# Gate and up projection of an encoder block by Strassen's seven products instead of eight

## The chip, the cores and the metric

The kernel runs on one core of a Trainium2 chip. The metric is the device time of one execution in microseconds. A profile of one execution gives, for each engine, every instruction's start and length; TensorE (PE) multiplies, VectorE (DVE), ScalarE (ACT) and GpSimd (POOL) work element by element, SyncE (SP) issues the DMAs. PEld are PE's weight loads, which overlap its products.

## The reference

One layer of a hybrid encoder block, 512 tokens of width 1024, in float32. The part that changes is its last third:

```python
mixed = (g_attn * attn_out + g_ssd * ssd_out) @ w_out[i]
x = x + rms_norm(mixed, norm1_post[i])
h2 = rms_norm(x, norm2_pre[i])
gate, up = jnp.split(h2 @ w_gate_up[i], 2, axis=-1)      # 1024 -> 2 x 2816
ffn = (jax.nn.silu(gate) * up) @ w_down[i]               # 2816 -> 1024
x = x + rms_norm(ffn, norm2_post[i])
```

Ahead of it stand the input projection, attention and a state-space branch, whose code the change leaves as it is.

## The kernel before

Every matrix product is made of float32r products in three passes: each operand is split into a high part (a cast on ACT, line 150 for weights, 187 for activations) and a low part (the difference, line 152 on DVE or POOL, 188 on DVE), and low x high, high x low and high x high are added in PSUM (`mm3`, lines 182 to 184).

Weights come in chunks of 128 x 1024 through a ring of three buffers `raw`, and their parts lie in rings `whi` and `wlo` of four buffers each. `wnext` hands out chunks in the order of use and splits AHEAD = 2 of them early. Activations lie in rings of 2 KB slots (`SLOTS`: x, z, q, t). PSUM has eight banks, in four rings of two (sa, sb, mm, sc). A planner with a cost model sets the order of each engine's instructions from the order of the trace in which the program lists them and from their dependencies; within `manual_schedule` the named engines keep the listed order. Once set, an engine's order is fixed.

`out_proj` computes the output projection token tile by token tile (four tiles of 128) into all eight banks (`token_major8`); the last four of the eight k-tiles are done one token tile after the other, so each tile's epilogue (two squares on ACT, rstd, residual sum, gain) runs beside the next tile's products. The epilogue ends with `transpose_tile`, eight PE transposes whose results are split into h2T. The row factor rstd is left out of h2T and multiplied in later, as a row `rb` that PE spreads over the partitions.

`ffn` goes through 22 blocks of 128 features. A block has a gate chunk and an up chunk of weights; each is multiplied with h2T of all 512 tokens (`chan_major`, 8 k-tiles x 3 passes = 24 products of 512 columns). The first two blocks are done in halves of 256 tokens, so that they can begin while token tiles 2 and 3 are still in their epilogue; their first three weight chunks are held in ring q (NQW). `post` multiplies both results with rb, applies SiLU, multiplies, and splits the result for the next product. `down` is the last projection, again by `token_major8`, with 22 k-tiles.

Of the kernel before, what the change touches and what calls it, by code (L numbers as in the profile page):

```python
# [38 lines left out]
NQW = 3  # chunks of w_gu held in ring q  # L39
# [7 lines left out]

class Halves:
    """[P, 1024] held as two [P, 512] tiles; a slice of columns lies in one of them"""
# [10 lines left out]
class Block:  # L60
    def __init__(self, ctx, tc, a, out):
# [3 lines left out]
        self.cp = pool("cp", 1)  # L65
        self.wp = pool("wp", 3)
        self.bp = pool("bp", 4)
        self.sp = pool("sp", 1)
        self.tp = pool("tp", 6)
# [9 lines left out]
    SLOTS = {"x": 14, "z": 8, "q": 15, "t": 17}  # L79

    def slot(self, tag, shape, dt=F32, name="s"):
        """a tile of up to 2 KB per partition from one of the rings"""
        return self.sp.tile([P] + list(shape), dt, tag=tag, name=self.nm(name), bufs=self.SLOTS[tag])

# [13 lines left out]
    def weights(self):  # L98
        """every weight chunk in the order of use: (source, columns, engine of the low parts)"""
# [16 lines left out]
        for j in range(NF):  # L116
            for u in range(2):
                yield a["w_gu"][j + u * NF], 1024, "g" if j < 3 and j > 0 else "v", 2 * j + u < NQW
        for j in range(NF):
            yield a["w_dn"][j], 1024, "v"  # L120

    def wload(self):
        c = next(self.wseq, None)
        if c is not None:
            src, n, lo, *q = c
# [10 lines left out]
    def presplit(self):  # L136
# [12 lines left out]
        for c in cs:  # L149
            self.A.copy(h[:, c], raw[:, c])  # L150
# [692 lines left out]
    def token_major8(self, nk, ntail, lhs, epilogue):  # L843
# [230 lines left out]
```

## Time and profile before

| | us |
|---|---|
| median of 3 runs (lowest to highest) | 870.79 (867.84 to 872.43) |
| span of the profiled execution, first to last instruction | 862.0 |
| from the span to the lowest, median, highest run | 5.8, 8.8, 10.4 |

The profile is of one execution, of which the span is known; the runs' times contain what lies around the span as well. A term worked out from the profile changes the span, and the 8.8 us are taken over to the median.

### The profile page before, as it was taken

To read this page: it belongs to the slowest core of one execution; us is meant where nothing else is said; L and a number is where in the kernel's file an instruction comes from. 1 tells how busy PE (TensorE), PEld (TensorE's weight loads), DVE (VectorE), ACT (ScalarE), POOL (GpSimd) and SP (SyncE) were. 2 spreads that over 40 slices of the span, in tenths; PEclk is the share of its full clock that TensorE was granted. 3 is DMA by queue.
4 is the path that set the end of the run, shared out by engine and by line. 5 is a ranking of instruction groups with operands and counts; after the bars stand their busy time and mean duration, and the time that the engine had idled before them with its cause. 6 is when DMAs were issued, how large, how long until landed. Compare 5 with 4: busy or idle time off the path is not lost.

```text
span 862.0 us, 10158 instructions
## 1 busy us (share of the span) xinstructions
PE 833.0 (97%) x3886; PEld 666.3 (77%) x3886; DVE 489.9 (57%) x730; ACT 337.1 (39%) x571; POOL 210.9 (24%) x124
## 2 busy tenths in 40 slices
PE   9898998799999999999999999999999999999996
PEld 7786886566666777677888798888888888888885
DVE  3976489876436667687863845444444444322225
ACT  7554445655723332276234624333333333211122
POOL 3454451400444465459451200000000000000000
PEclk9999999999999999999999999999999999999999
DMA  9422220200322221157225522222222222422214
GB/s 314 159 102 98 74 83 17 98 0 1 111 98 87 97 98 62 49 188 264 98 98 160 187 94 95 91 91 97 95 96 96 98 99 97 147 98 98 98 49 146
DMA packets 33312, 91.12 MB, mean 106 GB/s; under 512 B 4208, under 2 KB 4592, under 8 KB 33264
## 3 DMA queue, kind: packets, MB, share of 16 engines
q1 hardware_dynamic: 33264, 90.48, 30.5%
q8 instruction: 30, 0.49, 0.2%
q14 instruction: 18, 0.15, 0.1%
HBM read 82.08 MB, written 8.39 MB: 105 GB/s over the span
## 4 chain that ended last, share of the span: by engine, by line
PE 77%; DVE 12%; ACT 4%; issue 3%; DMA 2%; POOL 1%; SPq 0%; DVEq 0%; ACTq 0%; POOLq 0%
PE mm L182 12%; PE mm L184 12%; PE mm L183 12%; PE sc L183 7%; PE sc L184 7%; PE sc L182 7%; DVE u L552 3%; PE sc L652 2%; PE sb L182 2%; PE sb L183 2%; PE sb L184 2%; PE sa L183 2%; PE sa L182 2%; PE sa L184 2%; PE sb L631 1%
## 5 line engine op out<-in xcount | busy, mean ns | idle before, releaser
L150 ACT CAST whi<-raw 128x1024 fp32r<-128x1024 f32 (+3 forms) x126 | 128.2, 1019 | 253.7 <-PE sc L184 122.8
L152 POOL TENSOR_TENSOR wlo<-raw,whi 128x1024 fp32r<-128x1024 f32 (+3 forms) x62 | 141.6, 2289 | 230.8 <-ACT whi L150 228.9
L152 DVE TENSOR_TENSOR wlo<-raw,whi 128x1024 fp32r<-128x1024 f32 (+1 forms) x64 | 78.1, 1220 | 110.9 <-ACT whi L150 110.9
L182 PE MATMUL mm<-hT,wlo 128*128 128x512 f32 x176 | 73.4, 417 | 0.0
L183 PE MATMUL mm<-hT,whi 128*128 128x512 f32 x176 | 69.5, 395 | 0.0
L184 PE MATMUL mm<-hT,whi 128*128 128x512 f32 x176 | 69.3, 394 | 0.0
L182 PE MATMUL mm<-h2T,wlo 128*128 128x512 f32 (+1 forms) x176 | 66.8, 379 | 0.0
L183 PE MATMUL mm<-h2T,whi 128*128 128x512 f32 (+1 forms) x176 | 66.8, 379 | 0.0
L184 PE MATMUL mm<-h2T,whi 128*128 128x512 f32 (+1 forms) x176 | 66.8, 379 | 0.0
L182 PE MATMUL sc<-h2T,wlo 128*128 128x512 f32 x160 | 62.7, 392 | 0.0
L184 PE MATMUL sc<-h2T,whi 128*128 128x512 f32 x160 | 62.3, 389 | 0.0
L183 PE MATMUL sc<-h2T,whi 128*128 128x512 f32 x160 | 62.2, 389 | 0.0
L182 PEld LDWEIGHTS mm<-hT,wlo 128*128 128x128 f32 x176 | 33.4, 190 | 9.1 <-issue 2.5
L183 PEld LDWEIGHTS mm<-hT,whi 128*128 128x128 f32 x176 | 33.2, 189 | 8.6 <-issue 2.4
L184 PEld LDWEIGHTS mm<-hT,whi 128*128 128x128 f32 x176 | 33.2, 189 | 7.4 <-issue 0.5
L182 PEld LDWEIGHTS mm<-h2T,wlo 128*128 128x128 f32 x176 | 33.1, 188 | 6.3
L183 PEld LDWEIGHTS mm<-h2T,whi 128*128 128x128 f32 x176 | 33.1, 188 | 6.3
L184 PEld LDWEIGHTS mm<-h2T,whi 128*128 128x128 f32 x176 | 33.1, 188 | 6.1
L743 DVE TENSOR_TENSOR E<-E,cb 128x512 f32<-128x512 f32 x16 | 28.6, 1788 | 11.4 <-ACT E L742 11.4
L183 PEld LDWEIGHTS sc<-h2T,whi 128*128 128x128 f32 x160 | 30.0, 188 | 6.5 <-issue 0.2
L182 PEld LDWEIGHTS sc<-h2T,wlo 128*128 128x128 f32 x160 | 30.0, 188 | 6.5 <-issue 0.2
L184 PEld LDWEIGHTS sc<-h2T,whi 128*128 128x128 f32 x160 | 30.0, 188 | 6.2
(374 smaller groups left out, 1912.8 us busy)
## 6 DMA issues: line engine op xcount, KB each, us to landing
raw<-in_w_gu SPq DMA_DIRECT2D x44, 512.0 KB, 3.2
raw<-in_w_dn SPq DMA_DIRECT2D x22, 512.0 KB, 3.3
raw<-in_w_g SPq DMA_DIRECT2D x16, 512.0 KB, 3.3
raw<-in_w_xbc SPq DMA_DIRECT2D x12, 512.0 KB, 3.4
raw<-in_w_z SPq DMA_DIRECT2D x8, 512.0 KB, 3.2
spd<-spill SPq DMA_DIRECT2D x16, 256.0 KB, 2.0
raw<-in_w_sp SPq DMA_DIRECT2D x8, 512.0 KB, 4.0
raw<-in_w_o SPq DMA_DIRECT2D x8, 512.0 KB, 3.2
```

What stands on the lines that cost most here:

```text
L150: self.A.copy(h[:, c], raw[:, c])
L152: e.tensor_tensor(l[:, c], raw[:, c], h[:, c].bitcast(F32), ALU.subtract)
L182: self.T.matmul(o, ll, rh, start=first, stop=False)
L183: self.T.matmul(o, lh, rl, start=False, stop=False)
L184: self.T.matmul(o, lh, rh, start=False, stop=last)
L552: self.tap[j] = V.scalar_tensor_tensor(u[:, lo_o : lo_o + n], p[:, lo_i : lo_i + n], self.cw[:, j, k : k + 1], u[:, lo_o : lo_o + n], ALU. ...
L631: self.T.transpose(pp[:, t * P : t * P + P], prs[t][:, k * P : k * P + P], self.ident)
L652: self.T.matmul(po[i * HD : i * HD + HD, :], self.vt[:, k, g * HD : g * HD + HD], pts[h - 1 + i][k], start=k == 0, stop=k == NT - 1)
L743: V.tensor_tensor(E, E, cb[:, 0].unsqueeze(1).to_broadcast([P, 4, P]), ALU.mult)
```

## The change

Write h2 (without its row factor) as A with blocks A11, A12 (tokens 0 to 255; k 0 to 511 and 512 to 1023), A21, A22 (tokens 256 to 511), and a block's weights as B11, B21 (gate, the two halves of k) and B12, B22 (up). The eight block products of AB become seven (Winograd's form of Strassen's algorithm):

- sums of weights per feature block: P1 = B11 + B12, P2 = P1 + B22, P3 = B12 + B22, P4 = P2 + B21 (P1, P3 on POOL, P2, P4 on DVE), each split into high and low parts afterwards
- sums of activations, once: R1 to R4 from A11, A12 and the transposes of tiles 2 and 3 (`blocks`), each split; low parts of R3, R2 and R1 on POOL
- products, each of 4 k-tiles x 3 passes with 256 columns (`product`): v = B21 A12, u = B11 A11, then u continued by P2 R2 and later by P1 R1, px = P3 R3 continued by P4 A22, pw = B22 R4. Between the continuations DVE and ACT read the partial sums.

PE's order is written out by hand for output projection and gate/up projection: a block's order is B21, B11, P1 of the block before, P3, B22, P2, P4. The first two products of blocks 0 and 1, which need tiles 0 and 1 alone, come before tile 3's transposes, and tile 2's lie among them. Further: tile t's transposes follow the next tile's products (`rest`); weights of gate/up are no longer split ahead through `wnext` and ring q; the products of SiLU and up are kept unsplit and split in `down`; up is not multiplied by rb, which is made good in the last epilogue by the factor r2; the rings x, z, q and the transposed activations end with the mixing, and rings e (25 slots) and A (14 of 4 KB) take their place.

```diff
+        self.mp = pool("mp", 1)
+        self.early = ExitStack()
+        self.bp = self.early.enter_context(tc.tile_pool(name="bp", bufs=4))
+        self.sp = self.early.enter_context(tc.tile_pool(name="sp", bufs=1))
...
-    SLOTS = {"x": 14, "z": 8, "q": 15, "t": 17}
+    SLOTS = {"x": 14, "z": 8, "q": 15, "t": 17, "e": 25}
...
-        for j in range(NF):
-            for u in range(2):
-                yield a["w_gu"][j + u * NF], 1024, "g" if j < 3 and j > 0 else "v", 2 * j + u < NQW
-        for j in range(NF):
-            yield a["w_dn"][j], 1024, "v"
...
+        rest = None
         for t in range(NT):
             for n in range(2):
                 for k in range(nk - ntail, nk):
                     one(k, t, n)
-            epilogue(t, po[t])
+            if rest:
+                rest()
+            rest = epilogue(t, po[t])
+        return rest
...
+        self.blk = {n: [self.sp.tile([P, 4, 256], F32R, tag="A", name=self.nm(n), bufs=14) for _ in range(2)] for n in BLOCKS}
...
+        plain = {}
+        def part(name, t, src, lo):
+            hi, l = (b[:, :, t % 2 * P : t % 2 * P + P] for b in self.blk[name])
+            s4 = src.rearrange("p (k s) -> p k s", k=4)
+            A.copy(hi, s4)
+            lo.tensor_tensor(l, s4, hi.bitcast(F32), ALU.subtract)
+        def blocks(m, t):
+            p = []
+            for i in range(2):
+                p.append(self.ps(("sa", "sb", "mm", "sc")[t]))
+                for k in range(4):
+                    T.transpose(p[i][:, k * P : k * P + P], m[i][:, k * P : k * P + P], self.ident)
+            if t < 2:
+                for i in range(2):
+                    part(("A11", "A12")[i], t, p[i], V)
+                    f = self.slot("e", [512], name="af")
+                    A.copy(f, p[i])
+                    plain[t, i] = f
+                return
+            a11, a12 = plain[t - 2, 0], plain[t - 2, 1]
+            r = {n: self.slot("e", [512], name=n) for n in ("R1", "R2", "R3", "R4")}
+            V.tensor_tensor(r["R3"], a11, p[0], ALU.subtract)
+            part("R3", t, r["R3"], G)
+            V.tensor_copy(r["R2"], p[0])
+            V.tensor_tensor(r["R1"], p[1], r["R2"], ALU.subtract)
+            V.scalar_tensor_tensor(r["R2"], r["R1"], -1.0, a11, ALU.mult, ALU.subtract)
+            V.scalar_tensor_tensor(r["R4"], r["R2"], -1.0, a12, ALU.mult, ALU.subtract)
+            part("R4", t, r["R4"], V)
+            part("R2", t, r["R2"], G)
+            part("A22", t, p[1], V)
+            part("R1", t, r["R1"], G)
...
-            self.transpose_tile(m, self.h2T, t, "sa")
+            return lambda: blocks(m, t) if t != 2 else late.append((m, t))
+        late = []
+        rest = self.token_major8(KD, 4, lambda k: self.mT[k], epilogue)
+        return (lambda: blocks(*late[0])), rest
+    def product(self, dst, w, a, start):
+        ah, al = self.blk[a]
+        for k in range(4):
+            c = slice(k * P, k * P + P)
+            for i, (x, y) in enumerate(((w[1][:, c], ah), (w[0][:, c], al), (w[0][:, c], ah))):
+                self.T.matmul(dst, x, y[:, k], start=start and k == 0 and i == 0, stop=k == 3 and i == 2, skip_group_check=True)
+    def ffn(self, blocks2, blocks3):
+        V, A, G = self.V, self.A, self.G
+        self.act = []
+        def prepare(j):
+            raw = [self.wp.tile([P, 1024], F32, tag="raw", name=self.nm("raw")) for _ in range(2)]
+            for i in range(2):
+                self.load(raw[i], self.a["w_gu"][j, i])
+            b11, b12, b22, b21 = raw[0][:, :512], raw[0][:, 512:], raw[1][:, :512], raw[1][:, 512:]
+            w = {}
+            def split(src, dst, lo):
+                A.copy(dst[0], src)
+                lo.tensor_tensor(dst[1], src, dst[0].bitcast(F32), ALU.subtract)
+            w["B11"] = [self.slot("e", [512], F32R, "b11") for _ in range(2)]
+            wide = [[self.wp.tile([P, 1024], F32R, tag=s, name=self.nm(s), bufs=4) for s in ("whi", "wlo")] for _ in range(3)]
+            for n, (i, c) in {"B22": (0, 0), "B21": (0, 1), "P1": (1, 0), "P3": (1, 1), "P2": (2, 0), "P4": (2, 1)}.items():
+                w[n] = [t[:, c * 512 : c * 512 + 512] for t in wide[i]]
+            p = {n: self.slot("e", [512], name=n) for n in ("P1", "P2", "P3", "P4")}
+            G.tensor_tensor(p["P3"], b12, b22, ALU.add)
+            G.tensor_tensor(p["P1"], b11, b12, ALU.add)
+            split(raw[1], wide[0], V)
+            split(b11, w["B11"], V)
+            V.tensor_tensor(p["P2"], p["P1"], b22, ALU.add)
+            V.tensor_tensor(p["P4"], p["P2"], b21, ALU.add)
+            for n in ("P3", "P2", "P4", "P1"):
+                split(p[n], w[n], V)
+            return w
+        rb = None
+        ready, late = [], None
+        def finish(j, w, u, x7, pw, g):
+            self.product(u[:, :256], w["P1"], "R1", False)
+            up = self.slot("e", [512], name="up")
+            A.copy(up[:, :256], pw[:, :256])
+            V.tensor_tensor(up[:, :256], up[:, :256], u[:, :256], ALU.add)
+            V.tensor_tensor(up[:, 256:], x7, u[:, :256], ALU.add)
+            V.tensor_tensor(g, g, rb, ALU.mult)
+            A.activation(g, g, AF.Silu)
+            act = self.slot("t" if j < self.SLOTS["t"] else "e", [S], name="act")
+            V.scalar_tensor_tensor(act, up, -1.0, g, ALU.mult, ALU.mult)
+            self.act.append(act)
+        first = []
+        for j in range(2):
+            w = prepare(j)
+            v, u = self.ps("sb"), self.ps("sa")
+            self.product(v[:, :256], w["B21"], "A12", True)
+            if j == 0:
+                blocks2()
+            self.product(u[:, :256], w["B11"], "A11", True)
+            first.append((w, v, u))
+        blocks3()
+        rb = self.spread(self.row_rstd(self.xss, self.rstd, sqrt=True), "mm", "e")
+        for j in range(NF):
+            if j < 2:
+                w, v, u = first[j]
+            else:
+                w = prepare(j)
+                v, u = self.ps("sb"), self.ps("sa")
+                self.product(v[:, :256], w["B21"], "A12", True)
+                self.product(u[:, :256], w["B11"], "A11", True)
+            if late:
+                finish(*late)
+            g = self.slot("e", [512], name="g")
+            A.copy(g[:, :256], v[:, :256])
+            V.tensor_tensor(g[:, :256], g[:, :256], u[:, :256], ALU.add)
+            px, pw = self.ps("sc"), self.ps("mm")
+            self.product(px[:, :256], w["P3"], "R3", True)
+            x7 = self.slot("e", [256], name="x7")
+            A.copy(x7, px[:, :256])
+            self.product(pw[:, :256], w["B22"], "R4", True)
+            self.product(u[:, :256], w["P2"], "R2", False)
+            self.product(px[:, :256], w["P4"], "A22", False)
+            A.copy(g[:, 256:], px[:, :256])
+            V.tensor_tensor(g[:, 256:], g[:, 256:], u[:, :256], ALU.add)
+            late = (j, w, u, x7, pw, g)
+        finish(*late)
...
-            hi, lo = self.slot(tag, [S], F32R, "ach"), self.slot(tag, [S], F32R, "acl")
-            self.hilo(hi, lo, s)
...
-        for j in range(2, NF):
-            ps = []
-            for u in range(2):
-                with self.tc.issue_after(last_hi.ins):
-                    w = self.wnext()
-                p = self.ps(("sc", "mm")[j % 2])
-                self.chan_major(p, *w, self.h2T)
-                ps.append(p)
-            post(j, *ps)
...
+        split = {}
+        def lhs(k):
+            for i in range(k // 2 * 2, min(k // 2 * 2 + 4, NF), 2):
+                if i not in split:
+                    split[i] = hi, lo = [self.sp.tile([P, 2, S], F32R, tag="A", name=self.nm(n), bufs=14) for n in ("ach", "acl")]
+                    for e in range(2):
+                        A.copy(hi[:, e], self.act[i + e])
+                        V.tensor_tensor(lo[:, e], self.act[i + e], hi[:, e].bitcast(F32), ALU.subtract)
+            return [h[:, k % 2] for h in split[k // 2 * 2]]
...
+            r = self.rms_cols(po, sqrt=True, scale=r2)
+            V.tensor_tensor(r, r, r2, ALU.mult)
...
-        self.out_proj()
-        self.ffn()
+        self.early.close()
+        with self.tc.tile_pool(name="lp", bufs=1, reuse_waits="tile") as self.sp:
+            self.feed_forward()
+
+    def feed_forward(self):
+        with self.tc.manual_schedule(engines={mybir.EngineType.PE}):
+            self.ffn(*self.out_proj())
         self.down()
...
+    def pairs(m):
+        gt, up = m[:NF], m[NF:]
+        first, second = np.concatenate([gt[..., :512], up[..., :512]], 2), np.concatenate([up[..., 512:], gt[..., 512:]], 2)
+        return np.stack([first, second], 1)
```

## Rows read from the trace of the kernel before

**Rows 1.** the page: span, and each engine's busy time, share, instructions
```profile
span 862.0 us, 10158 instructions
...
PE 833.0 (97%) x3886; PEld 666.3 (77%) x3886; DVE 489.9 (57%) x730; ACT 337.1 (39%) x571; POOL 210.9 (24%) x124
```

**Rows 2.** windows: PE, PEld, DVE, ACT, POOL busy us, clock, DMA share, GB/s
```profile
75.00:80.00 5.00, 1.10 (x6) 1.10 (x6) 3.59 (x5) 2.70 (x4) 2.35 (x1) 0.89 0.40 126
...
80.00:85.00 5.00, 5.00 (x24) 4.11 (x22) 3.60 (x6) 1.54 (x4) 2.37 (x1) 0.77 0.42 151
...
360.00:400.00 40.00, 38.82 (x190) 29.39 (x189) 34.51 (x46) 26.12 (x47) 26.16 (x20) 1.00 0.57 184
...
520.00:735.00 215.00, 215.00 (x951) 178.01 (x950) 101.63 (x123) 65.84 (x82) 0.00 (x0) 1.00 0.28 98
```

**Rows 3.** timeline of PE, 256 columns, 33 steps between; start, length, what
```profile
492.73 0.28 PE L184 MATMUL sb<-h2T,qwh 128*128 128x256 f32 x1
...
496.68 0.28 PE L184 MATMUL sb<-h2T,qwh 128*128 128x256 f32 x1
```

**Rows 4.** timeline of PE, 512 columns; 960 products from first to second
```profile
517.17 0.79 PE L182 MATMUL sc<-h2T,wlo 128*128 128x512 f32 x1
...
735.21 0.39 PE L182 MATMUL sa<-whi,acl 128*128 128x512 f32 x1
```

**Rows 5.** timeline of PE, transition; in brackets idle before, releaser
```profile
476.29 0.40 PE L184 MATMUL sb<-whi,mTh 128*128 128x512 f32 x1
...
489.64 0.48 PE L184 MATMUL sc<-whi,mTh 128*128 128x512 f32 x1
...
492.02 0.63 PE L329 MATMUL sa<-cst,m 128*128 128x128 f32 x4 [1.91 <-DVE m L889]
```

**Rows 6.** groups by form, 520 to 735 us: count, busy, mean ns, idle
```profile
L152 DVE TENSOR_TENSOR wlo<-raw,whi 128x1024 fp32r<-128x1024 f32 x39 | 47.7, 1222 | 8.3 <-ACT whi L150 8.3
...
L150 ACT CAST whi<-raw 128x1024 fp32r<-128x1024 f32 x39 | 41.1, 1053 | 136.5 <-issue 73.2 <-PE mm L184 33.4 <-PE sc L184 30.0
...
L188 DVE TENSOR_TENSOR acl<-sg,ach 128x512 fp32r<-128x512 f32 x21 | 14.4, 685 | 0.1
...
L903 ACT ACTIVATE sg<-sg 128x512 f32<-128x512 f32 x22 | 13.8, 627 | 0.7 <-DVE sg L902 0.6
...
L902 DVE TENSOR_TENSOR sg<-mm,row 128x512 f32<-128x512 f32 x11 | 7.6, 691 | 22.1 <-PE mm L184 22.1
```

**Rows 7.** groups by form, whole run, POOL and DVE
```profile
L152 POOL TENSOR_TENSOR wlo<-raw,whi 128x512 fp32r<-128x512 f32 x8 | 10.3, 1296 | 12.9 <-ACT whi L150 12.9
...
L949 DVE SCALAR_TENSOR_TENSOR o<-o,ry,x 128x512 f32<-128x512 f32 x8 | 5.7, 750 | 0.1
```

**Rows 8.** line 459, min/median/max ns of 256-wide reads of PSUM
```profile
L459 DVE CAST kT<-sb x4: 409/410/418, 133.0 to 138.9; 128x256 fp32r<-128x256 f32 x4
...
L459 ACT CAST kT<-sb x4: 355/368/373, 134.7 to 139.6; 128x256 fp32r<-128x256 f32 x4
```

**Rows 9.** timeline of DVE: beside POOL, and without it
```profile
386.18 1.22 DVE L211 TENSOR_TENSOR rt<-ry 128x4 f32<-128x4 f32 x1
...
462.42 1.29 DVE L152 TENSOR_TENSOR qwl<-raw,qwh 128x512 fp32r<-128x512 f32 x2
...
482.02 1.29 DVE L889 TENSOR_TENSOR m<-xr,gn 128x512 f32<-128x512 f32 x2
...
488.43 3.45 DVE L889 TENSOR_TENSOR m<-xr,gn 128x512 f32<-128x512 f32 x2
...
502.51 0.16 DVE L211 TENSOR_TENSOR rt<-ry 128x4 f32<-128x4 f32 x1
```

**Rows 10.** timeline of POOL in two of these places
```profile
386.08 1.30 POOL L831 TENSOR_TENSOR at<-at,ga 128x512 f32<-128x512 f32 x1
...
488.80 5.34 POOL L152 TENSOR_TENSOR wlo<-raw,whi 128x1024 fp32r<-128x1024 f32 x2 [17.25 <-ACT whi L150]
```

**Rows 11.** timeline of PE, longest wait of an earlier stage
```profile
78.90 1.33 PE L570 MATMUL sa<-cst,u 128*128 128x128 f32 x5 [4.05 <-ACT u L554]
```

More of the change, by code (lines that the diff above doesn't have):

```diff
@@ L38 @@
 EARLY = 2
-NQW = 3
 PIN = 9
@@ L124, in wload @@
         if c is not None:
-            src, n, lo, *q = c
+            src, n, lo = c
             raw = self.wp.tile([P, 1024], F32, tag="raw", name=self.nm("raw"))
             self.load(raw[:, :n], src)
-            self.wraw.append((raw, n, lo, q and q[0]))
+            self.wraw.append((raw, n, lo))
     def wnext(self):
@@ L140, in presplit, with square_sum @@
             return False
-        raw, n, lo, q = self.wraw.pop(0)
+        raw, n, lo = self.wraw.pop(0)
         e = self.V if lo == "v" else self.G
-        if q:
-            h, l = (Halves([self.slot("q", [512], F32R, s) for _ in range(2)]) for s in ("qwh", "qwl"))
-            cs = (slice(0, 512), slice(512, 1024))
-        else:
-            h, l = (self.wp.tile([P, 1024], F32R, tag=s, name=self.nm(s), bufs=4) for s in ("whi", "wlo"))
-            cs = (slice(0, n),)
-        for c in cs:
-            self.A.copy(h[:, c], raw[:, c])
-        for c in cs:
-            e.tensor_tensor(l[:, c], raw[:, c], h[:, c].bitcast(F32), ALU.subtract)
+        h, l = (self.wp.tile([P, 1024], F32R, tag=s, name=self.nm(s), bufs=4) for s in ("whi", "wlo"))
+        self.A.copy(h[:, :n], raw[:, :n])
+        e.tensor_tensor(l[:, :n], raw[:, :n], h[:, :n].bitcast(F32), ALU.subtract)
         self.wready.append((h, l))
         return True
-    def square_sum(self, dst, src):
+    def square_sum(self, dst, src, scale=1.0):
         j = self.tp.tile([P, 512], BF16, tag="junk", name=self.nm("junk"), bufs=1)
-        self.A.activation(j, src, AF.Square, accum_out=dst)
+        self.A.activation(j, src, AF.Square, scale=scale, accum_out=dst)
     def row_rstd(self, ss, dst, sqrt=False):
@@ L863, in token_major8 @@
                     one(k, t, n)
[L864 removed]
+            if rest:
+                rest()
+            rest = epilogue(t, po[t])
+        return rest
     def out_proj(self):
[L867 to L869 removed]
+        V, A, G, T = self.V, self.A, self.G, self.T
+        self.blk = {n: [self.sp.tile([P, 4, 256], F32R, tag="A", name=self.nm(n), bufs=14) for _ in range(2)] for n in BLOCKS}
@@ L936, in down @@
-    def down(self):
-        V = self.V
-        g = self.gain("norm2_post", "z")
+            return lambda: blocks(m, t) if t != 2 else late.append((m, t))
[8 more added lines that the diff above has]
+                self.T.matmul(dst, x, y[:, k], start=start and k == 0 and i == 0, stop=k == 3 and i == 2, skip_group_check=True)
@@ new lines, in down @@
+    def down(self):
+        V, A = self.V, self.A
+        g = self.gain("norm2_post", "e")
+        self.wseq = ((self.a["w_dn"][j], 1024, "v") for j in range(NF))
+        split = {}
[7 more added lines that the diff above has]
+            return [h[:, k % 2] for h in split[k // 2 * 2]]
@@ L940, in epilogue @@
         def epilogue(t, po):
-            x = [self.slot("x", [512], name="x2") for _ in range(2)]
+            x = [self.slot("e", [512], name="x2") for _ in range(2)]
             for i in range(2):
                 self.load(x[i], self.x2_d[t][:, i * 512 : i * 512 + 512])
-            m = [self.slot("x", [512], name="o") for _ in range(2)]
-            r = self.rms_cols(po, sqrt=True)
+            m = [self.slot("e", [512], name="o") for _ in range(2)]
+            r2 = self.rstd[:, t : t + 1]
@@ L1048, in lay_out @@
         "w_o": g["w_out"].reshape(KD, P, D),
-        "w_gu": rows(g["w_gate_up"], P, KD)[:, 0],
+        "w_gu": pairs(rows(g["w_gate_up"], P, KD)[:, 0]),
         "w_dn": g["w_down"].reshape(NF, P, D),
```

55 lines of the change are left out of this document (10 added, 45 removed).

## The prediction

> **What bounds the kernel now.** I read the page first [rows 1]: TensorE (PE) is busy for 833.0 of 862.0 us, so what changes the time is PE work or a wait of PE. Then the windows by stage [rows 2]: from 520 to 735 us, the loop over the 22 feature blocks of gate and up, PE is busy in all of 215.00 us, while VectorE (DVE) has 101.63, ScalarE (ACT) 65.84 and GpSimd (POOL) nothing. The reader is to see that this stage has one bound, PE's products, and much room on the other engines. Then PE's timeline, for what a product costs by start-to-start distance (a record's own length overlaps the next). With 512 columns: the loop's 960 products begin at 517.17, and the product after them at 735.21 [rows 4], 218.04 / 960 = 0.2271 us each. With 256 columns, which the first two blocks use: 492.73 to 496.68 is 33 steps, 0.1197 us each [rows 3]. Half the columns cost 0.527 of the time, not 0.5, because about 0.012 us per product doesn't shrink. Last, the transition from the output projection: its last product starts at 489.64, PE waits 1.91 us until 492.02, and the first 256-column products start right behind [rows 5].
>
> **The products (the gain).** Before: 192 x 0.1197 + 960 x 0.2271 = 23.0 + 218.0 = 241.0 us. After: 22 blocks x 7 block products x 4 k-tiles x 3 passes = 1848 products of 256 columns, 1848 x 0.1197 = 221.2 us. Difference -19.8 us. In columns alone it would be an eighth, about 30 us; the fixed part of the extra products (1848 against 1152) takes a third of it back. One block is then 84 x 0.1197 = 10.05 us of PE. The 256-column rows have the same operands (a 128x128 split weight held, float32r columns moved), so I keep 0.1197 as it is. Continuing a sum in PSUM needs no extra PE instruction.
>
> **The other engines, per block.** DVE after: one 1024-wide low part (1.22), five 512-wide ones (0.685 each), the sums P2 and P4 and the product with the row of rstd (0.69 each), the closing three-operand one (0.75): 7.47 us, all with two SBUF inputs; and four half-width adds that read PSUM, at 0.41 each from the only 256-wide PSUM read, 1.64 [rows 6, 7, 8]. Sum 9.11 of 10.05 us. It is less in a row: two low parts back to back take 1.29, 0.65 each [rows 9]. Before, DVE had about half of the loop. ACT: 1.05 + 6 x 0.63 + 4 x 0.37 = 6.3 us [rows 6, 8], covered. POOL: two 512-wide sums at 1.30 = 2.6 us [rows 7], where it had none. The weight loads are the same 44 of 512 KB, so DMA stays at 98 GB/s [rows 2], covered.
>
> So DVE must end 9.1 us of work in each 10.05, in an order fixed beforehand, with PE waiting for it at several points. Two are close. The second product into u may only start when the first sum has been read by DVE; that read has some 4 us, as has the copy of px. P2 and P4 need buffers that the previous block's P1 product frees in the third place of PE's order, and are used in the sixth: between them lie two products, 2 x 1.44 = 2.9 us, for a cast (0.63) and a low part (0.69). That fits unless DVE is behind. The price of being behind is what I can't read off: nothing (DVE just keeps up) to POOL's whole 2.6 us added to DVE's 9.11. The nearest row is 360 to 400 us, where DVE is busy for 34.51 of 40 us and POOL for 26.16: PE still got 38.82, 3% lost [rows 2]. With a POOL of a quarter instead of two thirds I take about half of that, 0.16 us per block: +3.5 us (0 to 36).
>
> **Why POOL matters.** From 386 to 388 us DVE instructions of four elements take 1.22 us each (0.16 at 502.51, where POOL is idle), beside POOL instructions of 1.30 that begin 0.1 earlier [rows 9, 10]. At 488.43 two DVE instructions that otherwise take 1.29 (482.02) take 3.45, with POOL's two from 488.80 on [rows 9, 10]. A DVE instruction with two SBUF inputs stands still for all of a POOL instruction. The Trainium skill says so too (SBUF — State Buffer, section "SBUF: two separate sides"): the port pair of the two engines is an exclusive lock for a whole instruction, not a shared bandwidth. By that rule the loop's worst case is a DVE that loses every POOL microsecond, 894 us where my sum has 862; the trace agrees with the rule, and it speaks against this change.
>
> **The transition (the loss).** The last product of the output projection ends at about 490. What PE does next before was ready: w_gu chunks split ahead in ring q, tiles 0 and 1 transposed. After, four waits, bounded by chains:
> (a) The first B21 needs a whi/wlo buffer, and all four hold w_o until the last 2 us of the projection; cast 1.05 + low part 1.22 [rows 6] then end about 0.3 us late with an idle DVE, which is in its epilogue: 1.0 us (0 to 2).
> (b) Then four block products (5.8 us) and tile 2's transposes, then tile 3's, which need its epilogue. Tile 1's epilogue took from 476.7 to 483.3 [rows 5, 9], 6.6 us; with blocks of tile 2 (seven DVE instructions, about 4.9 us, where two were) among it I take 8: 1.5 us (0 to 4).
> (c) The next product needs R3 of tile 3: subtraction 0.69, cast 0.63, low part on POOL 1.30, handoffs, and the transposes and the rstd product fill a part: 3.0 us (1 to 5).
> (d) R4 and R2, further down the same DVE chain, with POOL's R3 in its way: 1.5 us (0 to 3).
> Together 7.0 (1 to 14) where 1.9 stood: +5.1 us. From 490 to the end of block 0 DVE has some 22 us to do (the epilogue's six wide ones 4.3, the blocks of tiles 2 and 3 9.9, the weights of blocks 0 and 1 2 x 1.22 + 7 x 0.69 = 7.3, small ones), and PE about 13 us (8 products, the transposes), which is why I do not take the low ends.
>
> **The clock.** After PE's 4.05 us wait before 78.90 [rows 11] the granted clock was 0.89 in that window and 0.77 in the next 5 us, a mix of both levels [rows 2]; that cost (1 - 0.77) x 5 = 1.2 us. With waits of about 3 us in a group I count one dip: +1.2 us (0 to 2.5).
>
> **Down projection.** The activation's split (0.63 on ACT, 0.69 on DVE per block) moves from the loop to here, beside 24 x 0.227 = 5.4 us of PE per k-tile; covered by a DVE that has one low part of 1.22 there [rows 6]; the first pair lies ready well ahead, and without that cover it would cost 1.3 us once. Its first banks are those of u: the newer is read by two DVE adds of 0.41 after the last product, behind three products (0.68): +0.6 us (0 to 1.5). One small multiplication more in the last epilogue: +0.2. SP's order holds loads that wait for raw buffers ahead of the epilogue's x rows; these loads' buffers come free early in the tail, so nothing.
>
> **Sum.** 862.0 - 19.8 + 5.1 + 1.2 + 3.5 + 0.8 = 852.8 us span. The median of the runs, 870.79, lies 8.8 us above the profiled span (5.8 to 10.4 over the three), so 861.6: 862 us, 1.0% faster.
>
> **Rivals.**
> 1. *The loop loses a little in every block* and eats the gain. 19.8 - 5.1 - 1.2 - 0.8 = 12.7 us are left for it, 0.58 us per block: at a period of 10.6 us the time is unchanged. For: DVE at 9.1 of 10.05 with waits between engines. Against: back to back it is nearer 8. Time 867 to 875. Chance 0.2.
> 2. *DVE becomes the bound through POOL's lock* (the other side). It decides from 0.78 us per block, a period of 10.83. With the whole 2.6 us: 9.11 + 2.6 = 11.71, 22 x 1.66 = +36 us, 894; with half of it, 877. For: [rows 9, 10]. Against: the four adds from PSUM and DVE's idle time can take POOL's turns. 876 to 894. Chance 0.2. The Trainium skill's rule above is this rival.
> 3. *The transition is covered and the loop runs at PE's pace*: -19.8 + 0.5, 843 span, 852. Against: DVE's 22 us. Chance 0.1.
> 4. *Half-width products cost more than 0.1197 with other partners*, so the algorithm saves nothing: at 0.130 the products would be 240 us, and the time about 881. Against: rows 3 hold for 192 products in a row (493 to 516). Under 0.02, counted in rival 2's chance.
>
> **Numbers.** My forecast has 0.5 (856 to 868). Half a per cent, 4.4 us, is about what a measurement of this kernel can tell from no change: faster below 866.4. Faster 0.45 + 0.1 = 0.55, same 0.05 + most of rival 1 = 0.22, slower 0.23. Range 853 to 881: rival 3's best end and rival 2's upper half are left out.
>
> **What would show it.** Right: 256-column products 0.12 us apart, a block every 10.1 to 10.4 us, DVE busy about nine tenths of the loop, PE waits of 5 to 9 us between 490 and 515. Wrong: PE waiting in each block for a low part, with DVE records of 1.2 to 2 us beside POOL's (rival 2); or a transition of over 14 us.

## The result and the profile after

The kernel became slower: 879.67 us, median of 4 runs (878.59 to 881.81), against 869.32 us (865.52 to 872.43, 4 runs) for the kernel before. The ratio is 1.0138, 95% interval 1.0096 to 1.0181. The forecast was 862; its range, 853 to 881, holds the time, its sign was wrong. The profiled span is 876.8 us where the sum gave 852.8 and before had 862.0 [rows 1].

The page of the kernel after, its busy line and, in 40 slices of 21.9 us, PE's busy tenths and granted clock:

```profile
span 876.8 us, 12111 instructions
...
PE 823.9 (94%) x4582; PEld 691.7 (79%) x4582; DVE 618.7 (71%) x944; ACT 408.8 (47%) x754; POOL 280.8 (32%) x169
...
PE   8898998799999999999999638999999999999996
...
PEclk9999999999999999999999958999999999999999
```

PE is busy 9.1 us less than before [rows 1], so products were saved, but the span is 14.8 us longer. The slices show where most of it lies: in two of them, the 23rd and 24th (482 to 526 us), where PE falls to 6 and 3 tenths and the clock, in the second, to 5. All slices behind them up to the last have 8 or 9.

Spans alone mislead by some us, because executions differ ahead of the change. The first product of the output projection, behind code that the change leaves as it is, starts at these times in before and after:

```profile
443.62 0.39 PE L182 MATMUL sa<-whi,mTl 128*128 128x512 f32 x1
```
```profile
444.91 0.39 PE L176 MATMUL sa<-whi,mTl 128*128 128x512 f32 x1
```

From there to the end it is 418.4 us before and 431.9 after, 13.5 more.

First the loop, from the start of one block to the next (PE's timeline), a window, and DVE's and POOL's groups by form from 560 to 720 us, 16 blocks:

```profile
546.65 0.28 PE L929 MATMUL sb<-A,wlo 128*128 128x256 f32 x1
...
556.73 0.28 PE L929 MATMUL sb<-A,wlo 128*128 128x256 f32 x1
```
```profile
600.00:640.00 40.00, 40.00 (x335) 40.00 (x335) 38.68 (x57) 22.90 (x44) 12.30 (x8) 1.00 0.32 104
```
```profile
L947 DVE TENSOR_TENSOR wlo<-P,whi 128x512 fp32r<-128x512 f32 x64 | 66.7, 1061 | 0.0
...
L955 POOL TENSOR_TENSOR P<-raw 128x512 f32<-128x512 f32 x16 | 27.4, 1715 | 0.0
```

A block takes 10.08 us, 84 products of 0.1200 each, and PE is busy in 40.00 of 40.00 us. DVE has 38.68 of 40, and its low parts take 1061 ns instead of 685 [rows 6], POOL's sums 1715 instead of 1296 [rows 7]: both engines lose time to each other, and PE doesn't notice. The loop does what the change was made for.

Now the transition. PE's timeline, all waits between the output projection and the loop:

```profile
486.29 0.66 PE L877 MATMUL sb<-cst,m 128*128 128x128 f32 x4 [0.66 <-DVE m L914]
...
492.83 0.39 PE L929 MATMUL sb<-A,wlo 128*128 128x256 f32 x1 [0.41 <-DVE wlo L947]
...
494.76 1.26 PE L877 MATMUL mm<-cst,m 128*128 128x128 f32 x8 [0.25 <-DVE m L914]
...
498.39 1.69 PE L929 MATMUL sa<-A,b 128*128 128x256 f32 x12 [2.37 <-DVE b L947]
...
507.02 0.55 PE L929 MATMUL sb<-A,wlo 128*128 128x256 f32 x1 [6.94 <-DVE wlo L947]
...
513.63 2.93 PE L929 MATMUL sa<-A,b 128*128 128x256 f32 x12 [3.71 <-DVE b L947]
...
526.36 2.05 PE L170 MATMUL mm<-diag,ones 128*128 128x512 f32 x2 [8.31 <-DVE diag L164]
...
537.86 0.39 PE L929 MATMUL sa<-R,wlo 128*128 128x256 f32 x1 [2.37 <-DVE g L1012]
```

25.0 us of waits stand where before had 1.91 [rows 5]. Each ends on DVE. What DVE did meanwhile (its timeline; below it SP's, with the one DMA that comes late, and ACT's, with the cast behind it):

```profile
502.06 2.49 DVE L947 TENSOR_TENSOR wlo<-P,whi 128x512 fp32r<-128x512 f32 x4
...
504.47 0.68 DVE L887 TENSOR_TENSOR R<-af,mm 128x512 f32<-128x512 f32 x1
...
505.67 1.21 DVE L947 TENSOR_TENSOR wlo<-raw,whi 128x1024 fp32r<-128x1024 f32 x1
...
508.56 1.24 DVE L160 TENSOR_SCALAR rv<-rv 128x4 f32<-128x4 f32 x1
...
522.49 3.72 DVE L164 TENSOR_SCALAR diag<-cst,rstd 128x128 f32<-128x128 f32 x3
```
```profile
498.40 0.33 SPq L102 DMA_DIRECT2D raw<-in_w_gu  x1
```
```profile
502.04 1.04 ACT L946 CAST whi<-raw 128x1024 fp32r<-128x1024 f32 x1 [0.79 <-DMA raw<-in_w_gu]
```

The 6.94 us end with the weights of block 1's first product (505.67). Their load was issued only at 498.40, the cast was begun at 502.04, and then DVE had four low parts of block 0's sums in front (502.06), which PE needs 25 us later. The 8.31 us end with four small diagonals that feed the product that spreads rstd; three of them take 3.72 us beside POOL's low parts and sums, and an instruction on four elements takes 1.24.

### The profile page after: what moved, and what is told of

The parts are those of the page before. It is cut to its first block, busy times and chain, and to the rows that moved or that the text cites. A ratio compares the mean times of both kernels' runs of the same rounds, so it can differ in the third digit from the quotient of the medians.

```text
span 876.8 us, 12111 instructions
## 1 busy us (share of the span) xinstructions
PE 823.9 (94%) x4582; PEld 691.7 (79%) x4582; DVE 618.7 (71%) x944; ACT 408.8 (47%) x754; POOL 280.8 (32%) x169
## 5 line engine op out<-in xcount | busy, mean ns | idle before, releaser
L145 ACT CAST whi<-raw 128x1024 fp32r<-128x1024 f32 (+3 forms) x85 | 85.0, 1003 | 76.6 <-PE sc L178 69.1
L947 DVE TENSOR_TENSOR wlo<-P,whi 128x512 fp32r<-128x512 f32 x88 | 85.6, 995 | 4.9 <-ACT whi L946 4.8
L146 DVE TENSOR_TENSOR wlo<-raw,whi 128x1024 fp32r<-128x1024 f32 (+1 forms) x26 | 32.2, 1239 | 69.4 <-ACT whi L145 69.3
L929 PE MATMUL sa<-R,whi 128*128 128x256 f32 x352 | 66.2, 286 | 0.0
L946 ACT CAST whi<-P 128x512 fp32r<-128x512 f32 x88 | 50.3, 620 | 14.8 <-PE mm L929 13.1
L929 PEld LDWEIGHTS sa<-R,whi 128*128 128x128 f32 x352 | 55.6, 194 | 0.0
L929 PE MATMUL sa<-R,wlo 128*128 128x256 f32 x176 | 50.3, 286 | 2.4 <-DVE g L1012 2.4
L929 PE MATMUL sa<-A,b 128*128 128x256 f32 x264 | 36.7, 290 | 6.1 <-DVE b L947 6.1
L955 POOL TENSOR_TENSOR P<-raw 128x512 f32<-128x512 f32 x22 | 37.0, 1681 | 10.6 <-PE sa L877 10.6
L929 PEld LDWEIGHTS sa<-A,b 128*128 128x128 f32 x264 | 34.4, 198 | 6.6 <-DVE b L947 6.6
```

What stands on the lines that cost most here:

```text
L145: self.A.copy(h[:, :n], raw[:, :n])
L146: e.tensor_tensor(l[:, :n], raw[:, :n], h[:, :n].bitcast(F32), ALU.subtract)
L929: self.T.matmul(dst, x, y[:, k], start=start and k == 0 and i == 0, stop=k == 3 and i == 2, skip_group_check=True)
L946: A.copy(dst[0], src)
L947: lo.tensor_tensor(dst[1], src, dst[0].bitcast(F32), ALU.subtract)
L955: G.tensor_tensor(p["P1"], b11, b12, ALU.add)
```

## The experiments

Each kernel differs from the kernel after by its diff, and each ratio is to the kernel before. "Waits" are the sum of PE's waits from 484 to 560 us in its timeline, as the eight lines above. The last column is read from the profiled execution, from the output projection's first product to the end. What stands ahead of that product is code that no edit touches, yet it starts anywhere from 443.6 to 451.4 us in these executions. Behind it they repeat well: after, l1 and l2 are alike up to block 4, and each of their eight waits agrees within 0.07 us. A ratio's interval is about 0.004 each way, 3.5 us; the last column tells smaller differences, but of one execution each. In an expectation a letter stands for what that expectation calls it.

| kernel | median, us | ratio (95%) | waits, us | from output projection, us |
|---|---|---|---|---|
| before | 869.32 | 1 | 1.9 | 418.4 |
| after | 879.67 | 1.0138 (1.0096 to 1.0181) | 25.0 | 431.9 |
| e1_rstd_late | 877.93 | 1.0133 (1.0098 to 1.0169) | 19.5 | 428.7 |
| e2_clock_kept | 877.48 | 1.0127 (1.0093 to 1.0161) | 5.8, the rest filled | 426.7 |
| e3_lows_on_dve | 877.96 | 1.0140 (1.0095 to 1.0184) | 21.7 | 426.9 |
| e4_early_sums | 877.12 | 1.0120 (1.0083 to 1.0156) | 21.4 | 428.5 |
| e5_all_four | 869.69 | 1.0027 (1.0001 to 1.0053) | 13.8 | 421.2 |
| e7_lows_copied | 878.04 | 1.0133 (1.0082 to 1.0185) | 21.5 | 427.6 |
| l1_third_sum | 887.46 | 1.0235 (1.0199 to 1.0271) | 25.0 | 439.1 |
| l2_sums_on_dve | 878.43 | 1.0138 (1.0096 to 1.0181) | 25.0 | 431.6 |
| p2_two_plain | 866.34 | 0.9990 (0.9974 to 1.0006) | 13.8 | 419.9 |
| p3_three_plain | 856.26 | 0.9869 (0.9845 to 0.9893) | 4.4 | 407.6 |
| p4_four_plain | 862.80 | 0.9938 (0.9915 to 0.9961) | 7.0 | 413.1 |
| q2_two_plain_early_row | 859.54 | 0.9893 (0.9862 to 0.9925) | 8.1 | 412.5 |
| q3_three_plain_early_row | 853.24 | 0.9847 (0.9815 to 0.9879) | 2.9 | 405.8 |
| q4_four_plain_early_row | 855.93 | 0.9847 (0.9814 to 0.9879) | 2.7 | 407.0 |

**e1: one wait taken away.** The product that spreads rstd is moved behind the first block's seventh product.

```diff
-        rb = self.spread(self.row_rstd(self.xss, self.rstd, sqrt=True), "mm", "e")
...
             late = (j, w, u, x7, pw, g)
+            if j == 0:
+                rb = self.spread(self.row_rstd(self.xss, self.rstd, sqrt=True), "sc", "e")
```

> The product that spreads the row of rstd is moved from behind tile 3's transposes to behind the first block's P4 product, where its row is first needed. In the changed kernel PE waits 8.31 us there for the diagonals. Theory A (PE's written order makes it stand before the diagonals while R3, done by 520.2, lies ready): the first R3 product starts at 520 to 521 instead of 527.4, the R4 product then waits for DVE until 524 to 527; 4 to 7 us shorter, about 870 to 872 us span. Rival B (DVE's total work sets the end of the transition and the diagonals only happen to come last): the wait moves to R4 and to the new place; 0 to 2 us shorter.

The 8.31 us are gone, and in their place PE waits for R3 and R4, 0.62 to 2.25 us at a time. In all its waits are 5.5 us less. The median shows no gain, the last column 3.2 us, between what the theory (4 to 7) and the rival (0 to 2) expected. Part of what PE waits for next was late anyway.

**e2: the clock held up.** 168 products (the identity times A11) into unused half banks fill the long waits. They are extra work that nothing reads.

```diff
+        def busy(bank, n):
+            for _ in range(n):
+                self.T.matmul(bank[:, 256:], self.identr, self.blk["A11"][0][:, 0], start=False, stop=True, skip_group_check=True)
```

> 168 products of 256 columns (identity times A11) are put into PE's order in front of the four longest waits (18, 55, 30, 65 of them, at 0.12 us each about the length of the waits), into unused halves of PSUM banks; nothing reads them. They keep PE busy, so that the granted clock should stay at 1.00 where it was 0.50 to 0.73 from 505 to 530. Theory C (the lower clock costs its own 8 us, the stage's length minus products, transposes and waits): 5 to 8 us shorter, 869 to 872 us span. Rival B (the end of the transition is set by DVE and POOL, and a slow PE is hidden behind them): 0 to 3 us shorter, the waits' ends where they were, only the products behind the last wait (527 to 541) faster.

Windows of this kernel, and of the kernel after for the same times:

```profile
515.00:520.00 5.00, 5.00 (x41) 4.80 (x41) 4.93 (x9) 1.65 (x4) 3.68 (x3) 0.96 0.20 58
...
520.00:525.00 5.00, 5.00 (x45) 5.00 (x44) 4.83 (x12) 1.36 (x3) 1.29 (x1) 1.00 0.44 155
```
```profile
505.00:510.00 5.00, 2.90 (x12) 2.63 (x12) 5.00 (x8) 0.78 (x3) 4.13 (x3) 0.50 0.01 4
...
515.00:520.00 5.00, 3.04 (x16) 2.80 (x14) 4.66 (x10) 1.05 (x2) 1.13 (x1) 0.73 0.54 193
...
520.00:525.00 5.00, 0.00 (x0) 0.00 (x0) 5.00 (x7) 1.91 (x4) 4.39 (x5) 0.61 0.01 2
```

The clock is 0.96 and 1.00 where it was 0.73 and 0.61; from 510 to 515 us it still fell, to 0.70. In the kernel after, products at half clock cost up to 6.8 us (over the windows from 500 to 550, PE's busy time times what is missing of the clock). The ratio moves from 1.0138 to 1.0127, which can't be told from nothing; the last column falls by 5.2 us, as Theory C expected (5 to 8). Neither settles it. The planner set another order for DVE here (all four diagonals are done by 522.2 us), and PE was at the last fillers until 527.80, though POOL had ended R3's low part at 524.85. So the clock's share in the loss stays open. It can't be the main part, since it is at most these 6.8 us, and the span is 24.0 us above the forecast.

**e3 and e4: POOL's low parts moved to DVE; more buffers for the first sums.** R2 and R1 are edited as R3 is, the sums P1 to P4 as B11 is:

```diff
-            part("R3", t, r["R3"], G)
+            part("R3", t, r["R3"], V)
```
```diff
-            w["B11"] = [self.slot("e", [512], F32R, "b11") for _ in range(2)]
+            w["B11"] = [self.slot("t" if j < 2 else "e", [512], F32R, "b11") for _ in range(2)]
```

> The low parts of R1, R2 and R3 (tiles 2 and 3, six of 512 columns) are done by DVE instead of POOL. DVE gets 6 x 0.65 = 3.9 us of work more. Theory D (POOL's lock is what makes the transition long: DVE records of 0.6 to 1.8 us where 0.16 to 0.69 is usual, 8 us in all between 502 and 527): small DVE instructions return to 0.16 us, 3 to 6 us shorter. Rival E (DVE's own amount of work counts): 2 to 5 us longer, as the added work is larger than what the lock costs it.

> The split B11 and the four sums of blocks 0 and 1 are put into ring t, which has free slots by then, instead of ring e. Theory F (ring e of 25 slots is full with rows and gains of the epilogues, so the sums, the split of B11 and through them the weight buffers and loads of block 1 come late): the load of block 1's second chunk is issued some 10 us earlier than 498.4, the waits of 2.37, 6.94 and 3.71 us before the first products shrink to under half, 4 to 9 us shorter. Rival B (DVE's work sets the end in any case): those waits shrink, the later ones grow by as much, 0 to 3 us shorter.

In e3 most of the small instructions are back at 0.16 us, while DVE has six low parts more; waits 21.7 us, the last column 5.0 us less. DVE's busy time (third after the span's length) in the 40 us that begin 2.8 us ahead of the first gate product, in the kernel after and in e3:

```profile
490.00:530.00 40.00, 18.00 (x86) 14.94 (x85) 36.28 (x60) 16.45 (x35) 15.34 (x10) 0.72 0.24 85
```
```profile
494.20:534.20 40.00, 21.35 (x110) 18.03 (x109) 33.15 (x67) 17.67 (x38) 9.29 (x4) 0.66 0.26 87
```

DVE is busy 3.1 us less with 6 x 0.65 us of work more. So POOL's six low parts had lengthened DVE's instructions by about 7 us here (an estimate from these rows). In e4 the waits of blocks 0 and 1 become 4.17 and 3.59 us, and the one behind them grows (PE's timeline of e4):

```profile
524.06 2.05 PE L170 MATMUL mm<-diag,ones 128*128 128x512 f32 x2 [11.30 <-DVE diag L164]
```

What was done earlier on DVE pushed back what stood behind it; the last column falls by 3.4 us.

**e5: these three together, and DVE's order.** The edits of e1, e3 and e4, the copy of R2 on ACT, and, as the diff shows, the splits of blocks 0 and 1's sums listed behind tile 3's blocks:

```diff
+            def sums():
+                for n in ("P3", "P2", "P4", "P1"):
+                    split(p[n], w[n], V)
+            if j < 2:
+                w["sums"] = sums
...
         blocks3()
+        for w, _, _ in first:
+            w["sums"]()
```

> The edits that each gave 2 to 4 us of the transition are put together, with two more: rstd's product behind the first block, all low parts of R1 to R4 on DVE, sums of blocks 0 and 1 in ring t, the low parts of those sums traced behind tile 3's blocks, the plain copy into R2 on ACT. Theory B (the transition lasts as long as DVE's work from the last epilogue to R4 of tile 3 takes, with PE's order and POOL's lock only deciding where the wait shows): DVE's chain ahead of R3 and R4 loses some 12 us (P low parts 5.2, rstd and its diagonals 7, the copies 1.2), gains 3.9; about 10 to 14 us shorter than the changed kernel, span 862 to 867. Rival G (each edit only moved a wait and the next chain, loads and ACT, is as long): 4 us shorter as the best single one, span 872 to 874.

By the ratio some 10 us of the loss go, waits sink to 13.8 us, and the kernel is 0.3% above the one before. Alone, e1, e3 and e4 gave 3.2, 5.0 and 3.4 us in the last column, together 11.6; e5 gives 10.7. So it is no more than the sum of the three, and what the reordering and the copy on ACT add is not shown; neither was tried alone.

**e7: DVE's work taken away.** Low parts of the weights of blocks 0 and 1, of R1 to R4 and of A22 are plain copies on ACT: the differences are left out.

```diff
-            lo.tensor_tensor(l, s4, hi.bitcast(F32), ALU.subtract)
+            if name in ("R1", "R2", "R3", "R4", "A22"):
+                A.copy(l, s4)
```

> Leaves work out: the low parts of blocks 0 and 1 and those of R1 to R4 and A22 are plain copies on ACT instead of differences, so about 11.7 us of DVE work and six POOL instructions with their locks are gone from the transition, while PE's work and order stay. Theory B (DVE's amount of work sets the transition): 10 to 16 us shorter, span 861 to 867, DVE no longer busy all of 500 to 527. Rival G (loads, ACT and the order of PE set it): 0 to 5 us shorter.

By the ratio no gain; 4.3 us in the last column, where the theory expected 10 to 16. PE's and ACT's timelines, and a window with ACT busy in all of it (columns as in [rows 2]):

```profile
516.02 0.58 PE L932 MATMUL sb<-A,wlo 128*128 128x256 f32 x1 [10.96 <-ACT wlo L951]
```
```profile
509.63 1.04 ACT L949 CAST whi<-raw 128x1024 fp32r<-128x1024 f32 x1
...
514.92 1.05 ACT L951 CAST wlo<-raw 128x1024 fp32r<-128x1024 f32 x1
```
```profile
505.00:510.00 5.00, 0.06 (x1) 0.00 (x0) 5.00 (x10) 5.00 (x12) 2.51 (x2) 0.50 0.85 288
```

The same product, block 1's first, now waits 10.96 us for ACT. Between the two halves of its weight, at 509.63 and 514.92, ACT works off eight casts and copies for R and A22, which PE needs later. The work left DVE but went to ACT, so the run doesn't separate amount from order; it shows that ACT's queue, too, has things that PE needs later ahead of what it needs first.

**l1 and l2: how near the loop is to DVE's limit.** l1 adds a third, unused sum on POOL per block from block 4 on; l2 moves POOL's two sums to DVE.

```diff
+            if j > 3:
+                G.tensor_tensor(self.slot("e", [512], name="spare"), b11, b12, ALU.add)
```
```diff
+            (V if j > 3 else G).tensor_tensor(p["P3"], b12, b22, ALU.add)
+            (V if j > 3 else G).tensor_tensor(p["P1"], b11, b12, ALU.add)
```

> One more POOL sum of 512 columns per block from block 4 on (into a slot that nothing reads), 1.3 us of POOL and of its lock per block. In the changed kernel DVE is busy for 38.7 of 40 us in the loop, the waits for POOL included, and PE never waits. Theory H (DVE stands at its limit and my rival 2 was missed by a small margin): DVE needs about 1 us more than PE's 10.08 per block, 10 to 25 us longer, PE waits in each block. Rival I (DVE's records stretch beside POOL without costing it work, as it has room between them): 0 to 3 us longer.

> From block 4 on the two sums P1 and P3 are done by DVE instead of POOL: 2 x 0.65 us more work for DVE, no lock in the loop. Theory H (POOL's lock costs DVE nearly its whole 2.6 to 3.2 us): DVE is busy for less than before, about 36 of 40 us, and the time stays within 1 us since PE is the bound. Rival I (the lock costs DVE little): DVE's share rises from 0.97 to 1.00 and PE waits, 5 to 15 us longer.

Windows of l1, then of l2:

```profile
600.00:640.00 40.00, 39.39 (x324) 38.78 (x323) 39.44 (x53) 22.29 (x42) 20.45 (x12) 1.00 0.30 96
```
```profile
600.00:640.00 40.00, 40.00 (x336) 40.00 (x335) 36.75 (x65) 23.11 (x44) 0.00 (x0) 1.00 0.33 105
```

One more sum on POOL (1.3 us where nothing disturbs it [rows 7]) makes PE lose 12 products in 40 us (324 for 336) and the kernel 9.0 us against l2. Two sums more on DVE, with POOL idle, cost nothing: DVE is busy 36.75 us, less than the 38.68 with the sums on POOL. In the kernel after the loop holds, but with less than one POOL instruction per block to spare.

**p2, p3, p4: the transition without its work.** The first two, three or four blocks are worked out with eight products again (in halves of 256 columns, order as before the change); R1 to R4 are made beside them, their low parts on DVE as in e3. The rest keeps seven products.

```diff
+        def half(j, h, c):
+            w, pg, pu = plain[j]
+            s = slice(h * 256, h * 256 + 256)
+            a = f"A{h + 1}{c + 1}"
+            gate, up = ("B11", "B12") if c == 0 else ("B21", "B22")
+            four(pg[:, s], w[gate], a, c == 0)
+            four(pu[:, s], w[up], a, c == 0)
...
+        rb = self.spread(self.row_rstd(self.xss, self.rstd, sqrt=True), "mm", "e")
+        for j in range(2):
+            post(j)
+        self.sums(2)
+        self.sums(3)
+        for j in range(2, 3):
```

> The first three feature blocks are worked out with eight block products (three passes of 256 columns each, weights split whole, no sums of weights), the other nineteen with seven; R1 to R4 are made from copies of the transposed tiles beside blocks 0 and 1, all low parts on DVE. Nothing is left out. Theory A (the loss is DVE's queue between the output projection and the loop: the work that seven products need ahead of the first product): the waits of PE there sink from 24 us to 2 to 6 us, the clock stays, the loop keeps 10.08 us per block. Products 19 x 10.08 + 3 x 11.49 = 226.0 us instead of 241.0, -15.0, plus 1 to 4 of waits and 1 of the down projection: span 848 to 853, ratio to the kernel before 0.985 to 0.991. Rival B (the loss lies in the new order by hand and in the rings of buffers, whatever DVE has to do): waits of 10 us or more stay, ratio 0.997 to 1.01.

> The same with the first two blocks by eight products, twenty by seven. Theory A: -16.4 us of products, but DVE has some 33 us of work between 483 us and the first sums of weights' end, PE some 32: one or two waits of 1 to 4 us at the first block of seven; span 848 to 857, ratio 0.984 to 0.994. Rival B: ratio 0.995 to 1.01.

> The same with the first four blocks by eight products, eighteen by seven. Theory A: -13.6 us of products, DVE has slack, no wait over 1 us at the first block of seven; span 849 to 853, ratio 0.986 to 0.991, 1.4 us above three blocks if those are already covered. Rival B: ratio 0.998 to 1.01.

p3 came as expected: waits 4.4 us, 1.3% faster than before. p2 and p4 did not: 0.9990 where 0.984 to 0.994 was expected, 0.9938 where 0.986 to 0.991 was. DVE's timeline of p2 with its longest idle time there, and PE's with its longest wait:

```profile
523.48 0.69 DVE L1036 TENSOR_TENSOR g<-sa,row 128x512 f32<-128x512 f32 x1 [13.63 <-ACT row L172]
```
```profile
536.38 2.93 PE L943 MATMUL sa<-A,b 128*128 128x256 f32 x12 [8.98 <-DVE b L961]
```

In p2 DVE stands still for 13.63 us in front of the product with the row of rstd, which PE spreads only behind block 1; R1 to R4 wait behind it, and then PE waits 8.98 us for DVE. Amount or order was open at this point.

**q2, q3, q4: the same work in another order.** PE spreads the row one block earlier, and R1 to R4 are listed ahead of the posts:

```diff
-        for j in range(2):
-            for c in range(2):
-                half(j, 1, c)
+        for c in range(2):
+            half(0, 1, c)
         rb = self.spread(self.row_rstd(self.xss, self.rstd, sqrt=True), "mm", "e")
-        for j in range(2):
-            post(j)
         self.sums(2)
+        post(0)
+        for c in range(2):
+            half(1, 1, c)
         self.sums(3)
+        post(1)
```

> As the kernel with three blocks by eight products, but PE spreads the row of rstd behind block 0's second half instead of behind block 1's, and R1 to R4 are traced ahead of what follows the products of blocks 0 and 1. There DVE stood idle from 511.6 to 518.5 us, and PE then waited 1.49 and 1.46 us for DVE at 522.66 and 525.78. Theory A (DVE's queue): the idle time takes up R1 to R4 and the two waits go, span some 3 us shorter, 850 to 854, ratio to the kernel before 0.981 to 0.988. Rival: the first block of seven products at 540 is late then instead, since its sums come behind R1 to R4 in the queue; ratio 0.987 or above.

> Two blocks by eight products as before, but with the row of rstd spread behind block 0's second half and R1 to R4 ahead of the posts: the same instructions, another order. With the row late DVE stood still for 13.63 us (509.9 to 523.5), its next instruction in order being the product with that row, and PE waited 2.00, 2.12 and 8.98 us. If the order of DVE's queue sets the loss: the idle time takes up the 11 us of R1 to R4, the 8.98 us sink to 0 to 4, the time is 853 to 860, ratio to the kernel before 0.984 to 0.992. If the amount of DVE's work does: it has the same amount to do ahead of block 2's products, the waits stay at 9 us or more, ratio 0.995 to 1.002.

> Four blocks by eight products with the early row. With the row late PE waited 2.23 us and 3.30 us for DVE at block 2's start, the weights' low parts and R1 to R4 standing ahead of the posts there. If the order sets it: these two go or sink to 1.5 together, and the time lies 1 to 3 us above that of three blocks with the early row (1.44 us more of products), 853 to 858, ratio 0.983 to 0.990. If something else lengthens the kernel with four blocks: 860 or more, ratio above 0.992.

All three are lower, q2 and q4 by more than their intervals; q3's 0.2% against p3 is within them (1.8 us in the last column). q2 has p2's instructions and is 1.0% faster against before (0.9893 for 0.9990): the 8.98 us wait is gone, one of 5.33 us has come, more than the 0 to 4 that were expected. q4 falls from 0.9938 to 0.9847. q3 has the lowest time here, 853.24 us (852.17 to 858.12), and the same ratio as q4. Its page and PE's last two waits:

```profile
span 850.9 us, 12114 instructions
...
PE 821.2 (97%) x4618; PEld 691.2 (81%) x4618; DVE 600.0 (71%) x924; ACT 402.9 (47%) x740; POOL 261.6 (31%) x157
```
```profile
502.57 1.26 PE L877 MATMUL sc<-cst,m 128*128 128x128 f32 x8 [1.02 <-DVE m L928]
...
521.71 0.35 PE L1023 MATMUL sa<-A,wlo 128*128 128x256 f32 x1 [1.22 <-DVE act L1039]
```

DVE's work in it is about that of the kernel after (600.0 against 618.7 us busy); its order and its place are other ones.

## Why the prediction was wrong

Span against span, the forecast was -9.2 us and the measurement +14.8, 24.0 apart.

- *Products, -19.8.* Right: 1848 products at 0.1200 are 221.8 us against 241.0, -19.2.
- *Loop, +3.5 (0 to 36).* Nothing was lost; DVE does 38.68 us in 40, a little more than "nine tenths". Rivals 1 and 2 didn't come, but l1 shows that rival 2 is one POOL sum of 1.3 us away. The Trainium skill's page "SBUF — State Buffer" (section "SBUF: two separate sides") says that whichever of the two engines first starts an instruction that needs their shared ports has them for all of it, and the other stands. The trace agrees with such a lock (0.16 to 1.24 us for four elements). It doesn't bear out the worst case of rival 2: POOL waits as well, and of POOL's 2.6 us DVE pays some 1.5 (four low parts at 1061 for 685 ns).
- *Transition, "Together 7.0 (1 to 14) where 1.9 stood: +5.1".* This step failed. Behind the start of the first product at 492.83 the waits are 24.0 us, where before had 1.9 in all: +22.0, which is 16.9 more than forecast. The text had named the mark: "a transition of over 14 us"; the waits of 5 to 9 us that it expected between 490 and 515 are 13.7. I bounded each wait by the chain of the one result that it waits for: cast, low part, hand-off. But DVE and ACT work in a fixed order, and PE too. A result waits for all that is listed ahead of it, and that was DVE's whole backlog: I counted 22 us of work, where its busy time from 490 to 530 is 36 of 40 us. Some 7 of these are POOL's lock (e3), which I had priced for the loop, but for the transition only within wait (d), at 1.5 us. The load issued at 498.40 and the sums' low parts ahead of R3 are such neighbours, and neither is in a chain that I had followed. Wait (a), the one with a chain of its own, was right: 0.41 for 1.0 (0 to 2); it is counted with the stage's start below.
- *Clock, +1.2 (0 to 2.5).* Too small: by the rows up to 6.8 us. I had one dip; the clock stood at 0.50 to 0.73 from 505 to 530 us. How much of this waiting would have taken anyway, e2 leaves open.
- *Stage start.* The first product begins at 492.83, where before the output projection ended at 490.12 [rows 5], +2.7. Of this 1.3 stand ahead of the output projection's first product already. In p3, p4 and q3 one product behind unchanged code begins at 471.78, 475.72 and 469.50 us, so single executions differ by more than that ahead of the change.
- *Down projection, +0.8.* About right: from its first product to the end it is 131.4 us where before had 126.8, but 36 of the last gate and up products (4.3 us) now lie among its first ones. That leaves +0.4.

Along PE's timeline these make up 22 of the 24.0 us (16.9 waits, 5.6 clock, 2.7 start, 0.6 products, less 3.5 of the loop and 0.4 of the down projection). The rest is not separated; among it are eight transposes more behind the first product.

- *The offset.* I carried 8.8 us from the span to the median. In the four runs of the kernel after, time and span differ by 1.8 us (878.59 and 876.8). The profiled execution of before was thus a quick one, and 7 of the 8.8 us were the spread between executions. By luck it made the forecast of the median 6 us better than that of the span, and only so does the range hold the time.

Shown: the loop works as forecast (window, l2); the loss lies in the transition (p3 gives up 4.2 us of products there and takes the ratio from 1.0138 to 0.9869); the order of the queues can cost several us with the work unchanged (p2 to q2, p4 to q4). Not settled: how the 24 us split in the kernel after itself between the amount of DVE's work, its order, POOL's lock and the clock. The single edits give 3 to 5 us each, by one execution each. e5 kept 13.8 us of waits; q2, with less to do ahead of its first seven-product block, kept 8.1. More slots in ring e itself, with seven products from block 0 on, were not tried; e4 took the first sums' slots from another ring.

## What to carry to other kernels

An algorithm that saves products by preparing more must also be costed at its start: count all work that stands ahead of the first product on each engine, in the order in which its queue will do it, and set it against the work that PE has meanwhile. Where that doesn't fit, begin with a few blocks of the plain form and prepare beside them: three plain blocks cost 3 x 1.4 us of products and took away 22 us of waits (q3, with its order). The Trainium skill's page "Perfetto Trace Analysis" (section "Optimization Strategy") says that a kernel whose most contended engine changes over time may gain from interleaving such stretches. q3, which prepares beside plain blocks, agrees: 0.9847 of before, where the kernel after has 1.0138.

When mending one wait seems to bring nothing, read it also from an instruction ahead of which no code has changed. By the medians e1, e3 and e4 were worth nothing that could be measured, because the executions differ by several us ahead of the change; from the output projection on, each was worth 3 to 5 us, and together, with a reordering, 10 us by the medians too. Then look at what ends the next wait.

## What the hardware showed unexpectedly

- A product of 256 columns at half clock starts 0.213 us after the one before (528.84 to 530.12 in the kernel after, two groups of three), 1.78 times the 0.120 at full clock, not twice.
- Two sums moved from POOL to DVE lowered DVE's busy time, from 38.68 to 36.75 us in 40: DVE lost more to POOL's two sums than the sums cost it when it makes them itself.
- Beside a third POOL sum DVE's 1024-wide low part took 2319 ns in the mean (l1, 560 to 720 us) instead of 1217, the 512-wide ones 917 instead of 1061: the waiting moved to other instructions, as the order fell.
